# Modulation of the first mixer on TensorE strips, in a two-layer transformer trunk scheduled at build time

## The chip, the cores and the metric

The kernel runs on one core of a Trainium2 chip. Its time is device time in microseconds of one execution, as the median of the runs taken. The engines that matter are TensorE (PE in the profile, PEld its weight loads), VectorE (DVE), ScalarE (ACT) and GpSimd (POOL). SyncE (SP) issues the loads from DRAM.

## The reference

A trunk of two layers works on 512 tokens of 1024 features in float32. Each layer has a mixer and a gated feed-forward part, and each of these four sub-layers is modulated by a vector that depends only on the sequence:

```python
c_act = jax.nn.silu(c)
for l in range(DEPTH):
    mod = (c_act @ mod_w[l] + mod_b[l])[:, None, :]
    sh_m, sc_m, g_m, sh_f, sc_f, g_f = jnp.split(mod, 6, axis=-1)
    h = x * (1 + sc_m) + sh_m
    y = even_mixer(h, ...) if l % 2 == 0 else odd_mixer(h, ...)   # sparse and latent attention; stick-breaking attention
    x = layer_norm(DEEPNORM_ALPHA * x + (1 + g_m) * y, ln_mix_g[l], ln_mix_b[l])
    h = x * (1 + sc_f) + sh_f
    y = conv_ffn(h, ...)
    x = layer_norm(DEEPNORM_ALPHA * x + (1 + g_f) * y, ln_ffn_g[l], ln_ffn_b[l])
```

`mod` is the product of one row of 1024 numbers with a 1024 x 6144 matrix, so 6 parts of 1024 columns for each layer: shift, scale and gate of the mixer (parts 0, 1, 2) and of the feed-forward (3, 4, 5). The mixer of layer 0 cannot begin before parts 0 and 1 of layer 0 are there; part 2 is wanted at the end of its output projection, parts 3 and 4 at the start of the feed-forward.

## The kernel before

**How it is ordered.** The class `Plan` (L79 to L446) records every engine call in program order with its reads and writes. `schedule` then issues them as a list schedule: each engine takes the recorded operation with the lowest index plus `bias` among those that are ready by the plan's own prices (`price`, L200). Some calls are left open between engines: `nc.either` and `nc.lazy` record one operation for VectorE, GpSimd or ScalarE, and `worth` (L334) gives it to the engine that would finish first, after adding a `gain` in ns for GpSimd. `port` (L243) says which operations of VectorE and GpSimd hold the shared port and for which of them `worth` looks. In the trace every operation has the one line L446, in `emit`, so tiles are told by their names.

**Matmuls.** Most products are float32 split in two float32r parts, high and low, with three products (high-high, high-low, low-high). A weight tile `raw` is loaded, copied to its high part `whl` by ScalarE, and the low part is a subtraction on VectorE or GpSimd. `hl`, `h`, `qk`, `y`, `V` and `xres` are tiles of activations; `sc`, `tr`, `mm` and `md` are PSUM banks. A float32 product that is not split is carried out by TensorE as two instructions.

**The start** (L664 on) is a loop over the 8 blocks of 128 features. For block k two loads of 512 KB bring the columns of parts 0 and 1 (`y` from `in_m_dram`), another brings the transposed input, two more the weights of the first projection. The modulation is summed over 8 rows `r` of the loaded tile: ScalarE scales two (`y<-y,ca`, `ca` being silu(c)), GpSimd adds these (`xres<-y`), VectorE adds the other six, scaled, in one after another (`xres<-y,ca,xres`), and TensorE sums the 128 partitions in two products with a column of ones (`md<-ones,xres`). VectorE forms `A` and `B` from it, then `t = x A + B`; `h` is its high part (ScalarE) and low part (VectorE). 21 products of 128x512 into seven banks follow per block.

**Parts 2, 3 and 4 of layer 0** are computed by `mod_gate(0)` and `mod_cols(1)` while the rotary embeddings, index scores, top-k masks, latent projections and latent attention run. 48 loads of 256 KB (`mraw` from `in_mod_w_dram`, two buffers) are scaled and added to the tile `acc` by GpSimd (`mraw<-mraw,ca`, then `acc<-acc,mraw`), or in one instruction by VectorE; products with ones (`md<-ones,acc` for columns, `md<-acc,ones` for a gate that is wanted on all partitions) sum the partitions. Their bias is `MOD_BIAS` = 1560.

After them come the sparse attention, the first output product with its norm (`out_proj`), the feed-forward (`ffn_up` and the second output product), then layer 1 with the third and fourth output products. In an output product token tiles end one after another: gate, residual, norm, transposition by TensorE, `A` and `B`, the next `h`.

Of the kernel before, what the change touches and what calls it, by code (L numbers as in the profile page):

```python
# [20 lines left out]
P = 128  # L21
D = 1024
S = 512
# [31 lines left out]
# ns from the end of an instruction to the start of one that waits for it  # L55
# [14 lines left out]
# what each hold of the SBUF ports shared by VectorE and GpSimd waits for  # L70
# [8 lines left out]
class Plan:  # L79
    """Records engine calls in program order and issues them in the order of a list schedule.  # L80

    Dependences are those of the recorded order (by tile and region); a tag's tiles take
    their buffers in the recorded order, so the schedule cannot run out of buffers where
    the recorded order does not.
    """

    def __init__(self, nc):
# [11 lines left out]
        self.either = _Either(self, -200.0)  # L99
        self.lazy = _Either(self, -1020.0)  # L100
# [11 lines left out]
    # -- recording --  # L112
# [86 lines left out]
    # -- costs --  # L199
    def price(self, op):  # L200
# [42 lines left out]
    def port(self, op, e=None):  # L243
        """how an op holds the pair of SBUF ports that VectorE and GpSimd share"""
# [15 lines left out]
    # -- scheduling --  # L260
    def schedule(self):
# [21 lines left out]
        def offer(i):  # L283
            """op i has all its inputs; it can run once its new tiles have buffers"""
# [32 lines left out]
        def port_free(i, e):  # L317
            """when the pair of SBUF ports that VectorE and GpSimd share is free for op i"""
# [15 lines left out]
        def worth(i, e):  # L334
            """whether engine e would finish op i before any other that may run it"""
# [20 lines left out]
        def pe_time(op):  # L356
            """the time of a TensorE instruction at the clock that its activity allows"""
# [12 lines left out]
        while done < len(ops):  # L370
# [41 lines left out]
            op.start = clock[e]  # L412
            k = self.port(op)
# [35 lines left out]
class _Either:  # L449
    """Operations that several engines may run, whichever comes to it first."""  # L450
# [14 lines left out]
    def scale(self, out, src, by):  # L465
        """out = src * by, a column"""
# [3 lines left out]
    def norm(self, x, mean, scale, bias):  # L470
        """x = (x - mean) * scale in place; bias = -mean * scale"""
# [1162 lines left out]
```

## Time and profile before

| | us |
|---|---|
| median of 3 runs | 1408.58 (1407.68 to 1410.41) |
| profiled execution, span of its trace | 1414.6 |
| TensorE busy | 1337.3 (95%) |
| VectorE busy | 1102.1 (78%) |
| ScalarE busy | 727.8 (51%) |
| GpSimd busy | 333.9 (24%) |

The profiled execution has no time of its own beside its span; the span is 6.0 us above the median of the runs. Busy time sums the instructions of an engine, pipelined matmuls merged; shares are of the span. GpSimd's 333.9 us lie mostly in the first 385 us. The clock column of a stretch is the share of full speed that the throttle granted TensorE, 1.00 being 2.4 GHz and 0.50 being 1.2 GHz, as a mean over the stretch.

### The profile page before, as it was taken

How to read it: one execution, taken by the hardware profiler on the slowest of the kernel's cores; microseconds unless marked ns; L12 is line 12 of the kernel's file. 1: busy time of each engine (PE TensorE's matmuls, PEld its weight loads, DVE VectorE, ACT ScalarE, POOL GpSimd, SP SyncE). 2: the span in 40 equal slices, each digit the busy share in tenths (PEclk: the TensorE clock that was granted, in tenths of full speed). 3: DMA queues.
4: the chain of work that ended last, by engine and by line, in shares of the span. 5: the costliest groups of instructions: out<-in, count | busy, mean ns of one | idle time of the engine just before them, and what ended most of it. 6: DMA issues, size and time to landing. Idle time of an engine off the chain costs nothing.

```text
span 1414.6 us, 21212 instructions
## 1 busy us (share of the span) xinstructions
PE 1337.3 (95%) x7468; PEld 1131.9 (80%) x7468; DVE 1102.1 (78%) x2030; ACT 727.8 (51%) x1376; POOL 333.9 (24%) x311
## 2 busy tenths in 40 slices
PE   4888799999899999999999999999969999999997
PEld 3666577887788999888877888878858999998885
DVE  6997997789898888883485886777688889994347
ACT  4355566753544444443334886788344555564230
POOL 4575866623611111020040100100041000020000
PEclk9987888999999999999999999999989999999999
DMA  9422433254155444553412243321305323242331
GB/s 323 149 66 65 131 97 107 90 165 134 60 165 170 133 156 153 174 168 107 134 42 93 75 146 112 108 82 60 104 30 176 116 98 120 89 150 93 101 105 59
DMA packets 88458, 166.54 MB, mean 118 GB/s; under 512 B 11128, under 2 KB 13688, under 8 KB 88352
## 3 DMA queue, kind: packets, MB, share of 16 engines
q1 hardware_dynamic: 88064, 165.14, 37.2%
q8 instruction: 58, 0.95, 0.3%
q14 instruction: 48, 0.39, 0.1%
q10 hardware_dynamic: 288, 0.06, 0.0%
HBM read 158.80 MB, written 2.10 MB: 114 GB/s over the span
## 4 chain that ended last, share of the span: by engine, by line
PE 71%; DVE 14%; issue 4%; ACT 4%; DMA 4%; POOL 2%; SPq 0%; DVEq 0%; POOLq 0%; ACTq 0%
PE sc L446 38%; PE tr L446 16%; PE mm L446 13%; PE md L446 4%; DVE t L446 4%; DVE xres L446 2%; DVE row L446 2%; ACT t L446 2%; DMA raw<-in_wup_dram 1%; DVE h L446 1%; DVE acc L446 1%; ACT qk L446 1%; DMA mraw<-in_mod_w_dram 1%; DVE hl L446 1%; DVE st L446 1%
## 5 line engine op out<-in xcount | busy, mean ns | idle before, releaser
L446 PE MATMUL sc<-h,whl 128*128 128x512 f32 (+1 forms) x2076 | 422.8, 359 | 7.8 <-ACT h L446 4.7
L446 PEld LDWEIGHTS sc<-h,whl 128*128 128x128 f32 x2076 | 348.7, 194 | 63.5 <-ACT h L446 5.5
L446 ACT CAST whl<-raw 128x512 fp32r<-128x512 f32 (+1 forms) x352 | 213.4, 613 | 264.0 <-PE sc L446 154.6
L446 DVE TENSOR_TENSOR whl<-raw,whl 128x512 fp32r<-128x512 f32 x296 | 207.8, 709 | 109.4 <-ACT whl L446 107.9
L446 POOL TENSOR_TENSOR whl<-raw,whl 128x512 fp32r<-128x512 f32 (+1 forms) x77 | 105.5, 1379 | 476.3 <-ACT whl L446 325.9
L446 DVE SCALAR_TENSOR_TENSOR acc<-mraw,ca,acc 128x512 f32<-128x512 f32 x118 | 98.0, 831 | 14.0 <-DMA mraw<-in_mod_w_dram 13.1
L446 POOL TENSOR_TENSOR rs<-rs,nhalf 128x1 f32<-128x1 f32 (+1 forms) x19 | 14.3, 754 | 328.5 <-DVE rs L446 328.4
L446 PE MATMUL sc<-whl,t 128*128 128x512 f32 x252 | 67.4, 393 | 0.3 <-ACT t L446 0.3
L446 ACT ACTIVATE t<-t 128x512 f32<-128x512 f32 x84 | 52.7, 637 | 19.5 <-DVE t L446 19.1
L446 DVE TENSOR_TENSOR raw<-raw,raw 128x512 f32<-128x512 f32 x86 | 59.1, 688 | 4.3 <-DMA raw<-in_wup_dram 2.8
L446 PE MATMUL mm<-h,whl 128*128 128x512 f32 x204 | 60.2, 435 | 1.2 <-ACT y L446 1.2
L446 ACT ACTIVATE t<-t,rs 128x512 f32<-128x512 f32 x16 | 13.0, 815 | 90.9 <-DVE rs L446 90.8
L446 PEld LDWEIGHTS sc<-whl,t 128*128 128x128 f32 x252 | 47.1, 188 | 11.3 <-DVE t L446 0.7
L446 PEld LDWEIGHTS mm<-h,whl 128*128 128x128 f32 x204 | 42.1, 212 | 11.5 <-ACT y L446 1.7
L446 ACT CAST hl<-t 128x512 fp32r<-128x512 f32 (+1 forms) x74 | 44.7, 627 | 5.4 <-DVE t L446 4.9
L446 PE MATMUL mm<-hl,V 128*128 128x128 f32 (+5 forms) x342 | 45.7, 276 | 1.2 <-ACT hl L446 0.9
L446 PEld LDWEIGHTS mm<-hl,V 128*128 128x128 f32 (+1 forms) x342 | 39.0, 168 | 8.0 <-ACT hl L446 2.1
L446 PE MATMUL tr<-whl,t 128*128 128x512 f32 x168 | 43.2, 391 | 0.0
L446 PE MATMUL mm<-whl,t 128*128 128x512 f32 x168 | 43.0, 391 | 0.0
L446 DVE SCALAR_TENSOR_TENSOR xres<-y,ca,xres 128x256 f32<-128x256 f32 x48 | 36.6, 773 | 8.0 <-POOL xres L446 7.2
L446 PE MATMUL tr<-h,whl 128*128 128x256 f32 (+1 forms) x240 | 40.1, 315 | 2.5 <-POOL whl L446 1.6
L446 PE MATMUL sc<-y,h 96*128 96x128 f32 (+3 forms) x96 | 34.4, 470 | 7.6 <-ACT y L446 3.2
(388 smaller groups left out, 2976.6 us busy)
## 6 DMA issues: line engine op xcount, KB each, us to landing
raw<-in_wup_dram SPq DMA_DIRECT2D x176, 256.0 KB, 3.4
mraw<-in_mod_w_dram SPq DMA_DIRECT2D x160, 256.0 KB, 2.9
raw<-in_wdown_dram SPq DMA_DIRECT2D x88, 256.0 KB, 2.9
y<-in_m_dram SPq DMA_DIRECT2D x16, 512.0 KB, 7.2
raw<-in_w_out_dram SPq DMA_DIRECT2D x32, 256.0 KB, 2.6
raw<-in_wqk_dram SPq DMA_DIRECT2D x32, 256.0 KB, 3.0
row<-in_ln_dram SPq DMA_DIRECT2D x8, 512.0 KB, 4.0
raw<-in_wqkv_dram SPq DMA_DIRECT2D x16, 256.0 KB, 3.0
```

Of the source, the lines that this page charges most:

```text
L446: getattr(getattr(self.nc, op.eng), op.fn)(*op.args, **op.kw)
```

## The change

**Start.** `ca` becomes column 0 of `cab`, a tile of 32 columns of which 31 are zero. For each block, 8 float32 matmuls take `cab[:, r, :]` (32 columns) as stationary operand and 256 modulation columns as moving one. Row r goes to partitions 32 (r mod 4) on, so four lie in one group of column positions each. ScalarE copies the 128x256 result, and the same two products with ones sum the partitions. VectorE's six additions, ScalarE's two scalings and GpSimd's addition go.

**Parts 2, 3, 4 of layer 0.** `first_gate` and `first_cols` replace `mod_gate(0)` and `mod_cols(1)`. Each of the 48 loads feeds two strips (`md<-mraw,cab`), which add up in PSUM. The gate's four row pieces get the bias, which four small loads bring, and are spread over all partitions by four products; the columns are obtained by four transposes. `MOD_BIAS` is 200.

**Engines and order.** GpSimd's `gain` goes from -200 and -1020 to 9000 ns up to the first output product, from 390 to 2000 until layer 1's attention, where it stays 500, and from 840 to 9000 for `either` after it. The price of a float32r product becomes the longer of its streaming plus 13 ns (7 up to 64 columns) and 0.859 ns a stationary column; a strip is priced at a quarter of its streaming; the start of a VectorE or GpSimd operation waits in the plan for `port_free`. The bias of `token_sums` falls from 670 to 100. `ones` shrinks to one column that is broadcast, `negs` from 15 to 12 columns. Docstrings and comments go too.

```diff
-        self.either = _Either(self, -200.0)
-        self.lazy = _Either(self, -1020.0)
+        self.either = _Either(self, 9000.0)
+        self.lazy = _Either(self, 9000.0)
...
+            if size(lhs) == COLS:
+                op.work /= P // COLS
+                return op.work + 2.5
...
-            return max(op.work + 2.5, size(lhs) * (1.6667 if lhs.dtype == F32 else 0.835))
+            return max(op.work + (13.0 if size(lhs) > 64 else 7.0), size(lhs) * 0.859)
...
+            if e in ("vector", "gpsimd"):
+                op.start = clock[e] = max(clock[e], port_free(i, e))
...
-        for r in range(MV_SPLIT, 8):
-            nc.scalar.mul(row(r), row(r), ca[:, r:r + 1])
-            if r > MV_SPLIT:
-                nc.gpsimd.tensor_tensor(acc[:, 1, :], row(r), acc[:, 1, :] if r > MV_SPLIT + 1 else row(MV_SPLIT), ALU.add)
-        nc.vector.scalar_tensor_tensor(acc[:, 0, :], row(0), ca[:, 0:1], acc[:, 1, :], ALU.mult, ALU.add)
-        for r in range(1, MV_SPLIT):
-            nc.vector.scalar_tensor_tensor(acc[:, 0, :], row(r), ca[:, r:r + 1], acc[:, 0, :], ALU.mult, ALU.add)
+        for r in range(KD):
+            g = r % 4
+            nc.tensor.matmul(cs[COLS * g:COLS * g + COLS, 0:256], lhsT=cab[:, r, :], rhs=m0[r // 4][:, g, :], start=r < 4, stop=r >= 4, skip_group_check=True)
+        rk = xa[:, 1, 0:256]
+        nc.scalar.copy(rk, cs[:, 0:256])
...
-    TOPK_BIAS, MOD_BIAS = 1500.0, 1560.0
+    TOPK_BIAS, MOD_BIAS = 1500.0, 200.0
...
+    def strips(o, l, part, at):
+        for r in range(KD):
+            for half in range(2):
+                m = tl("mraw", [P, S])
+                nc.sync.dma_start(m[:], t["mod_w"][l, r * P:(r + 1) * P, part * D + half * S:part * D + (half + 1) * S])
+                for i in range(2):
+                    g = 2 * half + i
+                    nc.tensor.matmul(o[COLS * g:COLS * g + COLS, at:at + 256], lhsT=cab[:, r, :], rhs=m[:, 256 * i:256 * i + 256], start=r == 0, stop=r == KD - 1, skip_group_check=True)
...
-    drain([mod_gate(0), mod_cols(1)])
+    first_gate()
+    first_cols()
...
-            nc.bias = 670.0
+            nc.bias = 100.0
...
-    nc.either.gain, nc.lazy.gain = (390.0, -180.0)
+    nc.either.gain, nc.lazy.gain = (2000.0, -180.0)
...
-    nc.either.gain, nc.lazy.gain = (840.0, 410.0)
+    nc.either.gain, nc.lazy.gain = (9000.0, 410.0)
```

In the issue order of TensorE, one step of the start reads as follows before: `md<-ones,xres` are the two sums over partitions for the next block, all others products of the current one.

```order
L446 MATMUL md_99<-ones,xres_118 128x1 x2
L446 MATMUL tr_94<-h_91,whl_111 128x512
L446 MATMUL tr_95<-h_91,whl_111 128x512 x3
L446 MATMUL mm_96<-h_91,whl_112 128x512 x3
L446 MATMUL sc_97<-h_91,whl_112 128x512 x3
L446 MATMUL mm_98<-h_91,whl_112 128x512 x3
```

The same place after, where `md_100<-y_125,cab` are four strips of a later block.

```order
L454 MATMUL sc_93<-h_92,whl_112 128x512
L454 MATMUL md_100<-y_125,cab 32x256 x4
L454 MATMUL sc_93<-h_92,whl_112 128x512 x2
L454 MATMUL sc_94<-h_92,whl_112 128x512 x3
L454 MATMUL md_100<-y_126,cab 32x256 x4
L454 MATMUL tr_95<-h_92,whl_112 128x512 x3
L454 MATMUL tr_96<-h_92,whl_112 128x512
L454 MATMUL md_100<-ones,xres_127 128x1 x2
L454 MATMUL tr_96<-h_92,whl_112 128x512 x2
L454 MATMUL mm_97<-h_92,whl_113 128x512 x3
L454 MATMUL sc_98<-h_92,whl_113 128x512 x2
L454 MATMUL md_100<-y_133,cab 32x256 x4
```

Each block's two groups of four strips now stand singly between products, two to three blocks ahead of the products that need them.

On VectorE, one step of the start before: the additions of the modulation lie around `A`, `B`, `t` and `h`.

```order
L446 SCALAR_TENSOR_TENSOR A_77<-md_99,mbT 128x1
L446 TENSOR_TENSOR B_81<-md_99,mbT 128x1
L446 TENSOR_SCALAR t_48_131<-xres_126,A_77,B_81 128x512
L446 SCALAR_TENSOR_TENSOR xres_134<-y_132,ca,xres_134 128x256 x2
L446 TENSOR_TENSOR h_91<-t_48_131,h_91 128x512
L446 SCALAR_TENSOR_TENSOR xres_134<-y_132,ca,xres_134 128x256
L446 SCALAR_TENSOR_TENSOR xres_134<-y_133,ca,xres_134 128x256 x2
```

And after, where two subtractions of the weights `whl`, GpSimd's before, stand with `A`, `B`, `t` and `h`.

```order
L454 TENSOR_TENSOR whl_128<-raw_130,whl_128 128x512
L454 SCALAR_TENSOR_TENSOR A_78<-md_100,mbT 128x1
L454 TENSOR_TENSOR B_82<-md_100,mbT 128x1
L454 TENSOR_TENSOR whl_129<-raw_131,whl_129 128x384
L454 TENSOR_SCALAR t_48_132<-xres_127,A_78,B_82 128x512
L454 TENSOR_TENSOR h_92<-t_48_132,h_92 128x512
```

No addition of the modulation is left there, and the step has six instructions.

On TensorE at the first latent score (`sc<-y,h`), before: projections, then scores, with no modulation between them.

```order
L446 MATMUL sc_435<-h_333,whl_433 128x512 x9
L446 MATMUL sc_438<-h_333,whl_436 128x512 x6
L446 MATMUL sc_435<-h_333,negs 128x512 x2
L446 MATMUL sc_442<-y_439,h_333 128x128
L446 MATMUL sc_438<-y_439,negs 128x512
L446 MATMUL sc_438<-y_440,negs 128x512
L446 MATMUL sc_443<-y_440,h_333 128x128
L446 MATMUL sc_442<-y_439,h_333 128x128 x2
```

And after, where `md_341<-mraw_351,cab` is the pair of strips of one load.

```order
L454 MATMUL sc_431<-h_334,whl_429 128x512 x6
L454 MATMUL md_341<-mraw_351,cab 32x256 x2
L454 MATMUL sc_431<-h_334,whl_429 128x512 x2
L454 MATMUL sc_434<-h_334,whl_432 128x512 x6
L454 MATMUL md_341<-mraw_352,cab 32x256 x2
L454 MATMUL sc_431<-h_334,negs 128x512 x2
L454 MATMUL sc_438<-y_435,h_334 128x128
L454 MATMUL sc_434<-y_435,negs 128x512
L454 MATMUL sc_434<-y_436,negs 128x512
L454 MATMUL md_341<-mraw_353,cab 32x256 x2
L454 MATMUL sc_439<-y_436,h_334 128x128
L454 MATMUL sc_438<-y_435,h_334 128x128 x2
```

All 48 pairs stand ahead of the first sparse score, 11 of them ahead of the first latent score, 37 between the two; the sums of the partial sums are gone from there.

## Rows read from the trace of the kernel before

**Rows 1.** Busy time by stretches: us, PE, PEld, DVE, ACT, POOL (x instructions), clock

```profile
17.50:72.60 55.10, 50.11 (x203) 38.57 (x204) 50.62 (x87) 19.83 (x39) 28.18 (x23) 1.00 0.61 205
72.60:168.00 95.40, 81.04 (x311) 59.43 (x309) 83.11 (x154) 51.33 (x97) 71.28 (x57) 0.82 0.29 81
168.00:251.40 83.40, 75.61 (x445) 59.92 (x446) 71.00 (x194) 55.13 (x136) 53.10 (x64) 0.84 0.38 105
251.40:359.20 107.80, 106.11 (x700) 86.17 (x700) 91.07 (x244) 59.80 (x153) 45.47 (x53) 1.00 0.41 130
...
385.00:1010.00 625.00, 619.02 (x3393) 526.85 (x3392) 470.08 (x773) 349.06 (x617) 72.42 (x57) 0.99 0.40 125
```

**Rows 2.** Timeline of TensorE, first sums and product: start us, us, what [idle before]

```profile
14.40 1.01 PE L446 MATMUL md<-ones,xres 128*128 128x1 f32 x4 [14.40 <-DVE xres L446]
17.52 2.09 PE L446 MATMUL sc<-h,whl 128*128 128x512 f32 x4 [2.11 <-ACT h L446]
```

**Rows 3.** Timeline of ScalarE, first modulation rows

```profile
7.67 0.91 ACT L446 ACTIVATE y<-y,ca 128x256 f32<-128x256 f32 x2 [2.47 <-DMA y<-in_m_dram]
```

**Rows 4.** Timeline of TensorE, one k-step of the start

```profile
36.58 0.61 PE L446 MATMUL md<-ones,xres 128*128 128x1 f32 x4 [0.19 <-DVE xres L446]
37.05 1.19 PE L446 MATMUL tr<-h,whl 128*128 128x512 f32 x4
...
40.14 1.52 PE L446 MATMUL sc<-h,whl 128*128 128x512 f32 x6
...
42.65 0.49 PE L446 MATMUL md<-ones,xres 128*128 128x1 f32 x3 [0.54 <-DVE xres L446]
```

**Rows 5.** Timeline of VectorE, same step

```profile
38.29 1.00 DVE L446 SCALAR_TENSOR_TENSOR xres<-y,ca,xres 128x256 f32<-128x256 f32 x2
...
39.81 3.92 DVE L446 SCALAR_TENSOR_TENSOR xres<-y,ca,xres 128x256 f32<-128x256 f32 x4
```

**Rows 6.** Timeline of GpSimd, same step

```profile
40.85 2.61 POOL L446 TENSOR_TENSOR whl<-raw,whl 128x512 fp32r<-128x512 f32 x2
```

**Rows 7.** Groups by shape, GpSimd, 72 to 252 us: busy us, mean ns | idle before

```profile
L446 POOL TENSOR_TENSOR acc<-acc,mraw 128x512 f32<-128x512 f32 x23 | 29.4, 1278 | 3.0 <-DMA acc<-in_mod_b_dram 1.8
...
L446 POOL TENSOR_TENSOR whl<-raw,whl 128x512 fp32r<-128x512 f32 x9 | 13.3, 1479 | 8.5 <-DVE whl L446 4.9 <-ACT whl L446 2.1 <-DVE iwt L446 1.6
```

**Rows 8.** Groups by shape, VectorE, 72 to 252 us

```profile
L446 DVE TENSOR_TENSOR hl<-t,hl 64x512 fp32r<-64x512 f32 x4 | 6.3, 1579 | 0.1
...
L446 DVE TENSOR_TENSOR hl<-tr,hl 128x512 fp32r<-128x512 f32 x6 | 3.9, 681 | 0.5 <-ACT hl L446 0.5
```

**Rows 9.** Timeline of TensorE, float32 products of 512 columns

```profile
445.41 0.84 PE L446 MATMUL sc<-h,whl 128*128 128x512 f32 x3
446.09 1.02 PE L446 MATMUL md<-acc,ones 128*128 128x512 f32 x2
446.54 2.18 PE L446 MATMUL sc<-h,whl 128*128 128x512 f32 x7
```

**Rows 10.** Timeline of TensorE, products in two halves of the rows

```profile
853.94 0.49 PE L446 MATMUL mm<-row,qk 64*128 64x512 f32 x1
853.95 0.49 PE L446 MATMUL sc<-row,qk 64*128 64x512 f32 x1
854.37 1.20 PE L446 MATMUL sc<-whl,h 128*128 128x512 f32 x4
```

**Rows 11.** The tile of modulation weights, 140 to 340 us: who waited, us, times

```profile
  DMA mraw<-in_mod_w_dram: 13.8, 13
```

**Rows 12.** Groups by shape, TensorE, 251.4 to 359.2 us

```profile
L446 PE MATMUL md<-ones,acc 128*128 128x1 f32 x30 | 4.4, 249 | 0.4 <-DVE acc L446 0.4
```

**Rows 13.** Timeline of TensorE, first and third output product

```profile
362.64 0.62 PE L446 MATMUL tr<-h,whl 128*128 128x256 f32 x3 [1.57 <-POOL whl L446]
...
1051.90 0.90 PE L446 MATMUL sc<-ident,t 128*128 128x128 f32 x3 [7.16 <-DVE t L446]
```

**Rows 14.** Timeline of VectorE, third output product

```profile
1042.23 3.09 DVE L446 TENSOR_TENSOR h<-t,h 128x512 fp32r<-128x512 f32 x2
```

More of the change, by code (lines that the diff above doesn't have):

```diff
@@ L21 @@
 P = 128
+COLS = 32
 D = 1024
@@ L628, in tile_trunk @@
     nc.sync.dma_start(cT[:], t["cT"])
-    ca = const("ca", [P, KD])
-    nc.scalar.activation(ca[:], cT[:], AF.Silu)
+    cab = const("cab", [P, KD, COLS])
+    nc.vector.memset(cab[:], 0.0)
+    nc.scalar.activation(cab[:, :, 0], cT[:], AF.Silu)
+    ca = cab[:, :, 0]
+    heads = const("heads", [P, 4])
+    nc.vector.memset(heads[:], 0.0)
+    for g in range(4):
+        nc.vector.memset(heads[COLS * g:COLS * g + 1, g:g + 1], 1.0)
     mbT = const("mbT", [P, 12, KD])
@@ new lines, in first_cols @@
+    def first_cols():
+        lng, lnb = lnT[:, 0, :], lnT[:, 1, :]
+        o = bank("md")
+        for what in range(2):
+            strips(o, 0, 3 + what, 256 * what)
+        x = tl("acc", [P, S])
+        nc.scalar.copy(x[:], o[:])
+        o = bank("md")
+        for j in range(4):
+            nc.tensor.transpose(o[:, j * P:(j + 1) * P], x[:, j * P:(j + 1) * P], ident[:])
+        cols = o[:].rearrange("p (w a g r) -> p w g a r", w=2, a=2, r=COLS)[:, :, :, :, 0]
+        got = []
+        for what in range(2):
+            c = small([P, KD], tag="mc", bufs=4)
+            nc.vector.tensor_tensor(c[:].rearrange("p (g a) -> p g a", a=2), cols[:, what], mbT[:, 3 + what, :].rearrange("p (g a) -> p g a", a=2), ALU.add)
+            got.append(c)
+        sh, sc = got
+        nc.vector.tensor_scalar(sc[:], sc[:], 1.0, None, ALU.add)
+        nc.vector.tensor_tensor(A_col[1][:], sc[:], lng, ALU.mult)
+        nc.vector.tensor_tensor(sc[:], sc[:], lnb, ALU.mult)
+        nc.vector.tensor_tensor(B_col[1][:], sc[:], sh[:], ALU.add)
@@ new lines, in first_gate @@
+    def first_gate():
+        o = bank("md")
+        strips(o, 0, 2, 0)
+        x = tl("acc", [P, S])
+        nc.gpsimd.memset(x[:, 0:256], 0.0)
+        for g in range(4):
+            nc.sync.dma_start(x[COLS * g:COLS * g + 1, 0:256], t["mod_b"][0:1, 2 * D + g * 256:2 * D + (g + 1) * 256])
+        nc.vector.tensor_tensor(x[:, 0:256], o[:, 0:256], x[:, 0:256], ALU.add)
+        gate = tl("gate", [P, D])
+        gates[0] = gate
+        for half in range(2):
+            o = bank("md")
+            for i in range(2):
+                g = 2 * half + i
+                nc.tensor.matmul(o[:, 256 * i:256 * i + 256], lhsT=heads[:, g:g + 1].broadcast_to((P, P)), rhs=x[:, 0:256], start=i == 0, stop=i == 1, skip_group_check=True)
+            nc.scalar.activation(gate[:, half * S:(half + 1) * S], o[:], AF.Identity, bias=ones[:, 0:1])
@@ L1112, in tile_trunk @@
         0: [tuple(va[:, i, j, :] for i in range(2)) for j in range(NT)],
-        1: [tuple(negs[:, 3 + 4 * i + j:5 + 4 * i + j, :].rearrange("p a b -> p (a b)") for i in range(2)) for j in range(NT)],
+        1: [tuple(negs[:, 4 * i + j:2 + 4 * i + j, :].rearrange("p a b -> p (a b)") for i in range(2)) for j in range(NT)],
     }
```

42 lines of the change are left out of this document (21 added, 21 removed).

## The prediction, made before the changed kernel was run

> **What bounds the kernel now.** I read the busy time by stretches first [rows 1]. From 385 to 1010 us TensorE is busy 619.02 of 625.00 us, so nothing that GpSimd or VectorE does there can matter until it makes TensorE wait. The change has to act before 385 us and in the two tails of the output products. The reader should see three different stretches ahead of that. From 17.5 to 72.6 us, the start, VectorE (50.62) and TensorE (50.11) are equally busy. From 72.6 to 168 us VectorE is at 83.11 of 95.40 and GpSimd at 71.28, while TensorE, busy 81.04, is granted a clock of 0.82. From 168 to 251.4 us nobody is full: TensorE 75.61 of 83.40 at 0.84, VectorE 71.00, GpSimd 53.10. From 251.4 to 359.2 us TensorE is busy 106.11 of 107.80: there it is the bound.
>
> Next I read one k-step of the start on TensorE [rows 4]: the sums of the modulation start at 36.58 and again at 42.65, 6.07 us apart, and the second start waited 0.54 us for VectorE. Then the reason on VectorE and GpSimd [rows 5, 6]: two scaled additions 128x256 end after 1.00 us, but four of them take 3.92 us while GpSimd's subtractions run beside them, about 0.98 each instead of 0.50. The same stretching is in the groups of 72 to 252 us [rows 8]: a 64x512 subtraction takes 1579 ns where a 128x512 one, whose input lies on PSUM, takes 681.
>
> **The sum.** It is made against the profiled execution, whose span is 1414.6 us. The median of the timed runs, 1408.6, lies 6.0 below it, and I take 6.0 off at the end. A change under 0.2% (2.8 us) is what a measurement here cannot tell from none. Two unknowns decide: q, what a group of four strips costs TensorE in the start, and p, what a pair costs it later.
>
> *Price of a strip.* No row of before shows a matmul with 32 stationary columns. A float32 128x512 product is two TensorE instructions; between 445.41 and the end at 448.72 two of them stand among ten products [rows 9]. Ten products at 0.227 from start to start (six from 40.14 to 41.50 [rows 4]), the last one with its full 0.39, leave about 0.87, so 0.43 each. A strip moves half the columns in two such instructions: 0.43 alone. Four one behind another are 1.71, two are 0.85. If strips in different column groups run side by side, a group or a pair takes 0.43 (a pair then fills half the array, a group all of it). The nearest rows to such sharing are two 64-row products in different halves of the array [rows 10]: they start at 853.94 and 853.95 and last 0.49 each, so they run together, and the next full product starts 0.42 later where streaming alone wants 0.227. Sharing exists, and about 0.2 goes on the change to and fro. I take q = p = 0.63, by that row, and keep 0.43 and the serial 1.71 and 0.85 as ends.
>
> The Trainium skill, TensorEngine Tiling (Array Packing), Key Properties, says that changing the tiling mode (not just the tile) drains TensorE; it speaks against putting 64 groups and pairs singly between full products, and the 0.42 for 0.227 in [rows 10] agrees in direction. The skill's TensorE: Matmul & The Clock Gate, Measured speedup vs the span model, has four row tiles at 3.07 times one after another and column tiles nearly alike; by it a group would be an estimated 0.56, which would make the sum about 3.5 us lower.
>
> *Start.* Removed per k: six VectorE additions, two ScalarE scalings, one GpSimd addition. Added: eight strips and one ScalarE copy of 128x256; VectorE takes GpSimd's two weight subtractions (about 0.6 and 0.5 at plain speed), far less than the 4.9 that go, so its cover is large and I cost it at nothing. The first product started at 17.52, behind a sum that waited until 14.40 for VectorE [rows 2], though the first modulation rows had landed at 7.67 [rows 3]: VectorE's six additions lay between. Two groups of strips and a copy take about 3 us there, so the first product starts some 3.8 us earlier. Against that, six groups come while products still run at half clock, each 0.43 dearer: 2.6. Net -1.2. For the seven later steps the 0.54 wait goes and two groups come: 7 x (2q - 0.54). Together T1 = 14q - 5.0; with 0.63 that is +3.8, with 0.43 +1.0. That the strips are in time rests on loads: a k's strips stand two to three steps ahead of its products.
>
> *72.6 to 251.4 us.* GpSimd is busy 124.4 there, of which modulation is 45 (its largest group 29.4 [rows 7]); 80 us of subtractions, rotations and scalings move to VectorE, where the same forms take half (681 against 1479 [rows 7, 8]). That is about 22 us more for VectorE before 168 and 15 after. What it gains is the stretching: its groups at their plain durations would be about 20 and 11 us shorter (four 64x512 subtractions alone give 3.6). So it goes from 83 to 86, and from 71 to 75. Before 168 it had 12.3 us of idle, mostly behind TensorE and ScalarE; I let 6 stay: 91.4 for 95.4, -4, between +3 (all idle stays) and -9 (none). The 11 pairs that stand before the first latent score lie under VectorE's work and cost nothing. After 168, TensorE's 445 instructions at their warm spacings are 58 us (75.61 at clock 0.84 gives 63.5 as the other end); 37 pairs come between the first latent score and the first sparse one, and 6 of the 7.8 idle stay: 58 + 6 + 37p against 83.4, so -19.4 + 37p, but not under -3.4, where VectorE's 75 and its 5 of idle bind. With 0.63, +3.9. T2 = -0.1. This counts on the full clock: the wait for GpSimd's products goes, TensorE is busier, and 83.4 at 0.84 becomes a stretch at 1.00 like the one behind it [rows 1]. If it stays at 0.84, up to 6 us are lost.
>
> *251.4 to 359.2 us.* The 30 small products of the partial sums [rows 12] go, at a spacing of 0.47 / 4 [rows 4] 3.5 us, with a wait of 0.4: T3 = -4, between 0 and -6.
>
> *Tails.* In the first output product TensorE waits 1.57 for a GpSimd subtraction [rows 13], and the gate is ready long before: -3 with two smaller waits. In the third it waits 7.16 at 1051.90 for VectorE [rows 13], at the end of a chain in which two subtractions took 3.09 us together beside GpSimd [rows 14]; plain they take half: -2. T4 = -5, between 0 and -8.
>
> Elsewhere the subtractions that leave GpSimd add about 35 us (half of GpSimd's 72.42) to VectorE's 470.08 of 625 [rows 1]: hidden by TensorE, and priceless until VectorE is late for a weight. The shorter constants and the other biases I cost at nothing under the same cover; with it gone they are a few tenths.
>
> Forecast: 3.8 - 0.1 - 4 - 5 = -5.3; 1414.6 - 5.3 - 6.0 = **1403 us**.
>
> **Rivals.** *Full sharing (q = p = 0.43).* The change of groups costs nothing: the rows show its price only for groups of rows, none for groups of columns. T1 = +1.0, T2 = -4 - 3.4, then -9: -15.4, 1393 us. Against it: 0.42 for 0.227 in [rows 10].
>
> *No sharing (q = 1.71, p = 0.85): slower.* One mechanism: a strip is two instructions that add into the same columns, and if TensorE starts each only when the one before has streamed its 256 columns, a group costs four strips. Place: the start, where TensorE has no idle to hide them, 7 steps of 2 groups, and the stretch after 168 us. T1 = 18.9, T2 = -4 + 12.1, -9: +18, 1427 us. It decides once q and p pass about 0.73 together (14q - 5 - 23.4 + 37p = 9). The rows show sharing only of single-pass products in halves of rows, not of float32 in columns, so it keeps a fair chance.
>
> *Half sharing (q = 1.27, p = 0.84).* A strip's second instruction waits for its first, but overlaps the next strip's first, with the 0.2 on top: T1 = 12.8, T2 = -4 + 11.7, -9: +11.5, 1420 us.
>
> *The queue.* Strips stand in TensorE's order and wait there for their load. In before, 13 waits for modulation weights cost GpSimd, ScalarE and VectorE 13.8 us together [rows 11] and TensorE next to nothing; the tile still has two buffers. If all of it moves to TensorE with the forecast's prices: -5.3 + 13.8, 1417; by half, 1410, no change. Against: the loads are issued as early as buffers come free, and strips free them within 1 us where GpSimd held one for 2 (1.278 for its addition alone [rows 7], after a scaling).
>
> **Chances.** Forecast 0.37, full sharing 0.25, none 0.15, half 0.13, the queue 0.10. The forecast's own range is 1397 to 1409 (the ends of T2 and T4), so a tenth of the whole from it is within 0.2% and nearly none slower; half of the queue's is. Faster 0.57, same 0.13, slower 0.30. The range of 8 in 10, from full sharing with somewhat more gained in the tails to no sharing without the upper tail: 1387 to 1425.
>
> **What would show it.** In the profile after, strips of a group starting within a few ns and the next product 0.6 after the group's first: q right; 0.43: full sharing; starts 0.2 apart through the group: none. First product near 13.7. Steps of the start 6.8 apart. TensorE's clock 1.00 from 168 us on, with VectorE busy near 75 there and its 64x512 subtractions near 680 ns: T2 right; 1579 still: the stretching has another cause than GpSimd. TensorE idle behind a modulation load of over 5 us in all: the queue. Idle at the third output product still over 6: T4 wrong. Times above 1411 would mean that strips cost more than the waits they replace.

## The result and the profile after

The changed kernel takes 1421.7 us (1412.1 to 1427.9, nine runs) where the kernel before took 1408.6 (1407.4 to 1410.6): a ratio of 1.0091, 95% interval 1.0070 to 1.0113. It is slower by 13 us; forecast were 1403 us and a gain. The profiled execution spans 1422.8 us and took 1424.6 as timed, 1.8 more than its span.

Stretches by work are compared below, cut at the same instructions in both kernels: the first product, the last product of the start, the first and the last latent score, the first product of the first feed-forward, the first of layer 1's projections, its attention, the third output product, its last transposed product, and the first product of the last output product. The view is busy time by stretches, with columns as in [rows 1]. After:

```profile
11.90:73.20 61.30, 61.30 (x331) 42.73 (x332) 36.95 (x80) 25.37 (x51) 0.00 (x0) 1.00 0.66 227
73.20:148.50 75.30, 69.88 (x332) 47.85 (x330) 66.57 (x158) 40.81 (x79) 3.73 (x3) 1.00 0.47 130
148.50:255.20 106.70, 100.97 (x599) 66.79 (x599) 83.11 (x239) 59.81 (x146) 0.00 (x0) 0.84 0.40 113
255.20:402.70 147.50, 141.68 (x943) 120.41 (x942) 124.38 (x304) 85.50 (x197) 31.67 (x29) 0.99 0.27 83
402.70:610.60 207.90, 203.27 (x1287) 183.73 (x1285) 175.70 (x310) 96.04 (x167) 5.96 (x5) 1.00 0.52 159
610.60:742.60 132.00, 130.23 (x579) 106.33 (x580) 79.66 (x136) 45.48 (x80) 16.99 (x14) 1.00 0.34 107
742.60:1045.10 302.50, 292.62 (x1538) 240.48 (x1537) 219.93 (x373) 206.19 (x371) 23.96 (x24) 0.99 0.31 94
1045.10:1076.40 31.30, 24.07 (x178) 23.18 (x178) 28.06 (x46) 16.53 (x31) 9.48 (x8) 0.84 0.19 58
1076.40:1292.30 215.90, 211.64 (x1435) 195.82 (x1434) 190.60 (x339) 113.59 (x200) 2.60 (x3) 0.99 0.39 122
```

And before, cut at the same work:

```profile
17.50:76.20 58.70, 53.71 (x219) 41.57 (x220) 54.22 (x89) 21.04 (x41) 31.70 (x25) 1.00 0.59 197
76.20:168.00 91.80, 77.44 (x295) 56.43 (x294) 79.51 (x152) 50.12 (x95) 67.76 (x55) 0.81 0.29 81
168.00:251.10 83.10, 75.31 (x443) 59.89 (x444) 71.00 (x194) 54.84 (x134) 52.87 (x63) 0.84 0.38 105
251.10:405.70 154.60, 147.71 (x974) 124.61 (x973) 133.39 (x303) 84.26 (x194) 70.13 (x70) 0.98 0.38 120
405.70:609.30 203.60, 201.84 (x1286) 183.34 (x1284) 174.62 (x293) 96.45 (x167) 23.53 (x19) 1.00 0.51 161
609.30:741.40 132.10, 131.69 (x581) 106.69 (x582) 81.20 (x131) 46.12 (x81) 24.78 (x18) 1.00 0.34 106
741.40:1038.80 297.40, 291.96 (x1537) 240.28 (x1535) 219.15 (x372) 204.21 (x368) 25.91 (x24) 0.99 0.31 96
1038.80:1074.10 35.30, 25.87 (x177) 24.28 (x176) 31.79 (x51) 19.08 (x33) 14.16 (x11) 0.81 0.23 71
1074.10:1284.10 210.00, 209.66 (x1435) 194.94 (x1434) 187.02 (x325) 111.49 (x198) 12.59 (x9) 1.00 0.37 122
```

The reader should see two halves. Up to the first feed-forward the changed kernel is ahead by 3 us (402.7 against 405.7), though GpSimd does next to nothing: the start ends 3 us earlier, the stretch up to the first latent score is 16.5 shorter, the latent stretch 23.6 longer, the rest 7.1 shorter. Two executions cannot carry these sizes alone. In the runs e4 and e14 below all engines keep the order of before up to some 327 us, and the start ends at 74.7 us in both (76.2 above) and the latent stretch at 245.4 and 247.8 (251.1 above). In e15 and e1 TensorE keeps the order of the changed kernel beyond 300 us, and the latent stretch ends at 248.9 and 248.2 (255.2 above). One order thus varies by 6 us there; the mean lead of three executions each at the first feed-forward is still 2.8 us (399.2 against 402.0), though their plans part after 306 us. From 402.7 on it loses 4.3 in the feed-forward, 5.1 in layer 1's attention, 5.9 in the second feed-forward, and wins 4.0 in the tail of the third output product. TensorE has idle there that it had not before: 207.90 less 203.27 is 4.6 where before it was 1.8, and 302.50 less 292.62 is 9.9 where it was 5.4.

*The strips.* The timeline of TensorE after, in the start and in the latent stretch:

```profile
35.10 0.64 PE L454 MATMUL md<-y,cab 128*32 128x256 f32 x8
35.67 0.96 PE L454 MATMUL mm<-h,whl 128*128 128x512 f32 x3
36.47 0.63 PE L454 MATMUL sc<-h,whl 128*128 128x512 f32 x2
...
40.48 0.40 PE L454 MATMUL tr<-h,whl 128*128 128x512 f32 x1
40.81 0.64 PE L454 MATMUL md<-y,cab 128*32 128x256 f32 x8
...
198.11 0.63 PE L454 MATMUL md<-mraw,cab 128*32 128x256 f32 x4
198.67 0.96 PE L454 MATMUL sc<-h,whl 128*128 128x512 f32 x3
...
218.45 1.07 PE L454 MATMUL md<-mraw,cab 128*32 128x256 f32 x4
219.45 1.01 PE L454 MATMUL sc<-y,h 96*128 96x384 f32 x2
```

Eight instructions are four strips. Their first instructions start within 20 ns, the second ones 0.24 us later, and the next full product 0.57 after the first (35.10 to 35.67): the four run side by side. The last product ahead of a group takes 0.33 to it (40.48 to 40.81) instead of 0.227. The first product behind a group is late too: three products take 0.80 (35.67 to 36.47), not 0.68. A group of four therefore costs 0.57 + 0.10 + 0.11 = 0.78 us among full products at the upper clock, and a pair 0.77 (0.56 from 198.11 to 198.67, with the same 0.10 and 0.11 where products of 128x512 stand on both sides). The Trainium skill, TensorE: Matmul & The Clock Gate, The mechanism, has row tiles starting some 4 ns apart; these column tiles start 6 to 7 ns apart in the trace. At half clock the pair takes 1.00 (218.45 to 219.45).

*The start.* The first product stood at 17.52 [rows 2]; now, from the timeline of TensorE:

```profile
11.88 0.79 PE L454 MATMUL sc<-h,whl 128*128 128x512 f32 x1
12.60 1.08 PE L454 MATMUL md<-y,cab 128*32 128x256 f32 x8
...
19.91 0.64 PE L454 MATMUL md<-y,cab 128*32 128x256 f32 x8
20.48 0.50 PE L454 MATMUL tr<-h,whl 128*128 128x512 f32 x1
```

It starts at 11.88. The group at 12.60 still takes 1.0 to the next product; from the one at 19.91 on it is 0.57. In before TensorE idled until 14.40, and its products still start 0.40 apart from 27.91 to 29.11, so the faster spacing comes some 9 us earlier now. The clock column reads 1.00 for the start in both kernels; the two speeds are read from the spacings.

*VectorE.* The group of VectorE from 73 to 255 us that stood at 1579 ns in [rows 8]:

```profile
L454 DVE TENSOR_TENSOR hl<-t,hl 64x512 fp32r<-64x512 f32 x4 | 2.7, 686 | 0.6 <-ACT hl L454 0.6
```

With GpSimd busy 3.73 us between 73.2 and 255.2, it takes what the 128x512 subtraction of [rows 8] takes, 681. The prediction named this as the sign that GpSimd caused the stretching.

*The clock.* Busy time at the second pair of heads, cut every 5 us:

```profile
170.00:175.00 5.00, 5.00 (x35) 3.19 (x32) 4.52 (x13) 2.27 (x4) 0.00 (x0) 1.00 0.39 108
175.00:180.00 5.00, 3.81 (x28) 1.97 (x26) 3.85 (x10) 3.25 (x6) 0.00 (x0) 1.00 0.70 206
180.00:185.00 5.00, 4.00 (x23) 2.12 (x21) 3.89 (x12) 2.56 (x8) 0.00 (x0) 0.82 0.57 161
185.00:190.00 5.00, 5.00 (x22) 3.38 (x22) 3.27 (x12) 2.65 (x9) 0.00 (x0) 0.50 0.36 105
```

TensorE is idle for 1.2 and 1.0 us in the second and third row, and in the fourth it is at 1.2 GHz (0.50). The whole latent stretch stands at 0.84, just as before.

*Tail of the third output product.* In [rows 13] TensorE waited 7.16 us; now 5.17:

```profile
1056.23 1.12 PE L454 MATMUL sc<-ident,t 128*128 128x128 f32 x4 [5.17 <-DVE t L454]
```

### The profile page after: what moved, and what is told of

It reads as the page before. It is cut to its first block, busy times and chain, and to the rows that moved or that the text cites. A ratio compares the mean times of both kernels' runs of the same rounds, so it can differ in the third digit from the quotient of the medians.

```text
span 1422.8 us, 21450 instructions
## 1 busy us (share of the span) xinstructions
PE 1361.0 (96%) x7764; PEld 1127.9 (79%) x7764; DVE 1070.7 (75%) x2105; ACT 726.7 (51%) x1380; POOL 97.8 (7%) x95
## 4 chain that ended last, share of the span: by engine, by line
PE 46%; DVE 13%; DMA 6%; ACT 4%; issue 4%; POOL 0%; DVEq 0%; POOLq 0%; ACTq 0%
PE sc L454 23%; PE tr L454 11%; PE mm L454 9%; DVE t L454 4%; DMA mraw<-in_mod_w_dram 3%; PE md L454 3%; DMA raw<-in_wup_dram 3%; DVE acc L454 2%; DVE whl L454 2%; ACT t L454 1%; DVE raw L454 1%; DVE row L454 1%; ACT qk L454 1%; DVE h L454 0%; ACT whl L454 0%
## 5 line engine op out<-in xcount | busy, mean ns | idle before, releaser
L454 ACT CAST whl<-raw 128x512 fp32r<-128x512 f32 (+2 forms) x351 | 212.3, 614 | 256.3 <-PE sc L454 147.7
L454 DVE TENSOR_TENSOR whl<-raw,whl 128x512 fp32r<-128x512 f32 (+1 forms) x344 | 231.7, 682 | 130.6 <-ACT whl L454 125.9
L454 DVE SCALAR_TENSOR_TENSOR acc<-mraw,cab,acc 128x512 f32<-128x512 f32 x104 | 79.6, 765 | 18.9 <-DMA mraw<-in_mod_w_dram 18.0
L454 POOL TENSOR_TENSOR whl<-raw,whl 128x512 fp32r<-128x512 f32 x29 | 42.7, 1479 | 371.0 <-DVE B L454 167.6
L454 DVE TENSOR_TENSOR raw<-raw,raw 128x512 f32<-128x512 f32 x92 | 63.5, 690 | 6.2 <-DMA raw<-in_wup_dram 4.5
L454 PE MATMUL mm<-h,whl 128*128 128x512 f32 x204 | 55.8, 404 | 0.7 <-ACT y L454 0.7
L454 PEld LDWEIGHTS sc<-whl,t 128*128 128x128 f32 x252 | 47.3, 188 | 10.7 <-ACT t L454 0.4
L454 ACT CAST hl<-t 128x512 fp32r<-128x512 f32 (+1 forms) x77 | 46.7, 625 | 10.6 <-DVE t L454 9.0
L454 PEld LDWEIGHTS mm<-h,whl 128*128 128x128 f32 x204 | 37.1, 188 | 12.4 <-issue 4.6
L454 ACT CAST hl<-tr 128x128 fp32r<-128x128 f32 (+3 forms) x64 | 26.1, 425 | 36.7 <-PE tr L454 36.2
L454 DVE TENSOR_TENSOR hl<-tr,hl 128x128 fp32r<-128x128 f32 (+3 forms) x64 | 30.1, 486 | 15.2 <-ACT hl L454 15.0
L454 DVE TENSOR_TENSOR hl<-t,hl 128x512 fp32r<-128x512 f32 (+1 forms) x44 | 29.4, 689 | 15.6 <-ACT hl L454 11.1
```

Of the source, the lines that this page charges most:

```text
L454: getattr(getattr(self.nc, op.eng), op.fn)(*op.args, **op.kw)
```

## The experiments

Theory L, formed on the profile: the loss is in the later stages because GpSimd was shut out of them and VectorE is late. Rival S: the strips and the half clock they meet make the loss. Rival P: it is the plan's new prices. All ratios are to the kernel before, measured beside.

| run | what it is | us | ratio (95%) |
|---|---|---|---|
| e1 | after, late gains and token bias of before | 1426.9 | 1.0147 (1.0115 to 1.0178) |
| e4 | before, late gains and token bias of after | 1407.1 | 0.9994 (0.9978 to 1.0010) |
| e2 | after, old prices, no port wait | 1408.9 | 1.0019 (0.9991 to 1.0048) |
| e6 | before, strips in the start, new prices | 1429.8 | 1.0159 (1.0131 to 1.0188) |
| e7 | before, strips in the start, old prices | 1409.7 | 1.0028 (1.0014 to 1.0042) |
| e8b | before, new product price | 1429.0 | 1.0162 (1.0144 to 1.0179) |
| e8c | before, port wait in the plan | 1427.0 | 1.0150 (1.0130 to 1.0170) |
| e9 | after, no port wait | 1432.0 | 1.0179 (1.0158 to 1.0200) |
| e10 | after, old product price | 1418.5 | 1.0071 (1.0041 to 1.0101) |
| e15 | after, old product price from the first output product on | 1407.9 | 1.0016 (0.9998 to 1.0034) |
| e16 | after, old product price up to there | 1419.7 | 1.0113 (1.0076 to 1.0150) |
| e11 | before, product 0.5 ns dearer | 1421.3 | 1.0093 (1.0067 to 1.0118) |
| e12 | after, other engines' prices 5% up | 1416.8 | 1.0061 (1.0040 to 1.0082) |
| e13 | e2, gain 840 after the third output product | 1409.6 | 1.0015 (0.9987 to 1.0043) |
| e14 | e4, gain 840 there | 1407.1 | 0.9992 (0.9979 to 1.0005) |
| e17 | e13, strips of parts 2 to 4 in fours | 1397.1 | 0.9933 (0.9917 to 0.9949) |
| e18 | after, strips in fours | 1408.7 | 1.0015 (0.9995 to 1.0034) |
| e19 | e15, strips in fours, gain 840 | 1402.2 | 0.9961 (0.9939 to 0.9982) |

**Gains and biases or prices.** The edits of e1 and e4 (reversed):

```diff
-    nc.either.gain, nc.lazy.gain = (2000.0, -180.0)
+    nc.either.gain, nc.lazy.gain = (390.0, -180.0)
...
-            nc.bias = 100.0
+            nc.bias = 670.0
...
-    nc.either.gain, nc.lazy.gain = (9000.0, 410.0)
+    nc.either.gain, nc.lazy.gain = (840.0, 410.0)
```

> Changed kernel with the settings of before from the first output product on (gains 390 and 840, token_sums bias 670). Theory L (the loss is VectorE being late there, once GpSimd is left out): the three stretches 403-610, 760-1045 and 1077-1292 us give back most of their 15 us, so 1407 to 1412 us. Rival S (strips at half clock and their waits make the whole loss, the late part is chance): 1418 to 1425, within 0.3% of the changed kernel.

> Kernel before with only the late settings of the changed one (2000 and 9000 ns, token_sums bias 100). Theory L: 8 to 15 us slower than before, 1417 to 1424. Rival S: within 0.3% of before, 1405 to 1413.

Theory L fell as the account of the whole loss, on both sides: giving the old settings back made it no faster (1426.9), and the new ones on the kernel before cost nothing (1407.1). The stretches say more than the sum. In e4's trace the second feed-forward takes 216.5 us instead of 210.0; in the changed kernel it takes 215.9, and in e1, with the old gains, 212.8. TensorE waits there for VectorE's `acc`, 3.5 us in e4 and 3.4 in the changed kernel, against 0.3 before. So this one loss goes with the late gain, as theory L has it. In e4 the attention of 294.2 us (297.4 before) and the tail of 31.5 (35.3) make up for it, and the attention by chance: in e14 TensorE keeps e4's order up to 1098 us and takes 297.4 for it, with 6.8 us at half clock that e4 does not have. The wait in the changed kernel (us in all, times, longest), then by stretches the attention of e4 and of e14 and the second feed-forward of e4:

```profile
PE md L454 <- DVE acc L454: 3.4, 2, 3.0
```

```profile
733.40:1027.60 294.20, 288.85 (x1537) 238.33 (x1535) 218.71 (x372) 204.10 (x368) 25.82 (x24) 1.00 0.30 96
735.27:1032.62 297.35, 291.98 (x1536) 240.21 (x1535) 218.87 (x372) 204.23 (x368) 25.84 (x24) 0.99 0.32 96
1059.10:1275.60 216.50, 211.95 (x1436) 195.89 (x1435) 190.15 (x337) 112.05 (x201) 6.16 (x5) 0.99 0.37 123
```

The edit of e2:

```diff
-            if lhs.dtype == F32:
-                return max(op.work + 2.5, size(lhs) * 1.6667)
-            return max(op.work + (13.0 if size(lhs) > 64 else 7.0), size(lhs) * 0.859)
+            return max(op.work + 2.5, size(lhs) * (1.6667 if lhs.dtype == F32 else 0.835))
...
-            if e in ("vector", "gpsimd"):
-                op.start = clock[e] = max(clock[e], port_free(i, e))
```

> Changed kernel with the prices of before (float32r product 2.5 ns over its streaming, no wait for the port when an operation starts in the plan). Theory L holds the gains to blame, so this stays within 0.4% of the changed kernel, 1416 to 1427. Rival P (the new prices make the plan believe that weights are ready when they aren't): 1408 to 1413.

Rival P held: 1408.9, with all strips and gains in place. Rival S falls with it as the whole cause; that the strips have a cost of their own is shown at the end. e6 and e7 are the kernel before with the start of the changed one, by the new and the old prices; seen from the changed kernel, beside the edits of e1 (and, in e7, e2):

```diff
-        self.either = _Either(self, 9000.0)
-        self.lazy = _Either(self, 9000.0)
+        self.either = _Either(self, -200.0)
+        self.lazy = _Either(self, -1020.0)
...
-    TOPK_BIAS, MOD_BIAS = 1500.0, 200.0
+    TOPK_BIAS, MOD_BIAS = 1500.0, 1560.0
...
-    first_gate()
-    first_cols()
+    drain([mod_gate(0), mod_cols(1)])
```

> Strips in the start alone: parts 2, 3 and 4 by vector sums, gains and biases as before, the new prices kept. If the start gains by itself what its traces show (-3 us at the end of the start) and the prices do nothing: 1403 to 1407. If strips cost more than they free there: 1409 or more.

> Kernel before with strips in the start alone and the old prices. The same with the new prices took 1429.8. If the prices are the whole of that loss: 1402 to 1408, the start's own 3 us gained. If the strips in the start have a part in it: above 1412.

1429.8 against 1409.7: 20 us from the prices. The second lies between its two answers: by the old prices the strips in the start gain nothing. The start ends at 75.7 us in e7 and at 72.6 in e6; against 76.2 both look like gains, against the 74.7 of e4 and e14, in before's order, e7's is none.

**Which price.** e8b and e8c put one each into the kernel before; e9 and e10 take one each out of the changed one (the first and the second hunk of e2's edit).

> Kernel before with only the new price of a float32r product (streaming plus 13 or 7 ns, 0.859 a column). Theory PP (the new product price alone makes the later stages slower, whatever the modulation): 1416 to 1424. Rival PW (it is the wait for the port in the plan): 1404 to 1410, no change. Rival X (the price hurts only together with strips): no change here and in the next.

> Kernel before with only the wait for the port when a VectorE or GpSimd operation starts in the plan. Theory PP: 1404 to 1410, no change. Rival PW: 1414 to 1422.

> Changed kernel without the wait for the port in the plan, the new product price kept. Theory PP: stays at 1417 to 1425. Rival PW: 1405 to 1412.

> Changed kernel with the old price of a product throughout and the port wait kept. Theory M: 1407 to 1413, like the one without the port wait (1408.9). Rival O: 1416 or more.

Either alone costs the kernel before 21 to 23 us, and the changed one keeps some 10 us or more over e2 while one of them is left, so neither theory was right alone. In layer 1's attention it is the product price: 300.6 (e8b) and 300.7 us (e9), against 294.0 in e8c and e10, all four without a stretch at half clock there. The same holds in the first feed-forward, 207.4 and 208.4 us against 203.0 and 203.6: in all twenty traces it takes 205.8 us or more where the new price holds there, and 204.8 or less where it does not. The port wait shows in the stretch that is 609 to 741 us in before: 138.1 us in e8c, 132.6 in e8b; but the changed kernel, which has it too, takes 132.0 there.

**Where the price acts.** In e15 and e16 a flag picks the old price for the operations recorded after, or before, the line that sets the gains for the first output product.

```diff
+            if getattr(self, "slim", False):
+                return max(op.work + 2.5, size(lhs) * 0.835)
             return max(op.work + (13.0 if size(lhs) > 64 else 7.0), size(lhs) * 0.859)
...
     nc.either.gain, nc.lazy.gain = (2000.0, -180.0)
+    nc.slim = True
```

> Changed kernel with the old price of a product from the first output product on only. Theory M (exact prices take the lead that operands had over TensorE; seen as idle of TensorE in the first feed-forward, 4.6 us for 0.3 to 1.8, and in layer 1's attention, 9.9 for 5.4): these two stretches give back 7 to 9 us, 1411 to 1416. Rival O (any plan but the one the settings were fitted to is late somewhere): 1418 or more.

> Changed kernel with the old price of a product up to the first output product only. Theory M: the late stretches stay as in the changed kernel (feed-forward 207.8, layer 1's attention 302.5), 1416 to 1424. If the early stages hold the harm: 1407 to 1413.

This is the clearest of the runs. Up to 306 us TensorE's instructions stand in the same order in both kernels, so only the later plan differs, and 1421.7 becomes 1407.9 (13.8 us between the medians, 10.6 by the two ratios to before). At one mean clock, 0.985, the changed kernel took 1419.5 us and e15 1406.9 and 1404.0, so the lower clock of some runs does not make the difference. Its stretches, first feed-forward to second, as above:

```profile
396.70:599.40 202.70, 202.10 (x1286) 183.27 (x1284) 176.23 (x305) 96.29 (x167) 15.22 (x12) 1.00 0.51 165
599.40:731.70 132.30, 131.29 (x584) 107.58 (x585) 78.97 (x136) 46.17 (x81) 14.41 (x13) 1.00 0.33 106
731.70:1028.80 297.10, 291.55 (x1534) 239.74 (x1532) 220.27 (x373) 205.31 (x371) 22.72 (x23) 0.99 0.31 95
1028.80:1060.60 31.80, 24.11 (x178) 23.21 (x177) 28.86 (x49) 18.70 (x33) 11.03 (x9) 0.84 0.17 53
1060.60:1274.30 213.70, 212.39 (x1436) 195.40 (x1435) 186.18 (x331) 112.45 (x198) 8.93 (x7) 1.00 0.38 124
```

207.9 has become 202.7, 302.5 is 297.1, 215.9 is 213.7; together 12.8 us. The two profiled spans differ by 18.0; the 6.0 us ahead of the first feed-forward fall almost whole where the order is the same, and are no effect of the edit. What TensorE waits for in layer 1's attention (us in all, times, longest), before, after and in e15:

```profile
PE mm L446 <- ACT hl L446: 1.3, 5, 0.4
```

```profile
PE mm L454 <- ACT hl L454: 3.3, 4, 1.2
PE mm L454 <- issue: 1.5, 1, 1.5
```

```profile
PE mm L456 <- issue: 1.5, 1, 1.5
PE mm L456 <- ACT hl L456: 1.1, 4, 0.4
```

With the new price 3.3 us are waited for ScalarE's copy `hl`, with the old one 1.3 and 1.1. That is 2 of the 5 us; the rest is spread over small waits. e16, with the new price late, stays slow. So does e10, which has e15's price late but another plan early; its runs go from 1409.6 us at a mean clock of 0.985 to 1426.4 at 0.970. The terms do not simply add up.

**How big the price must be.** Theory M: the old price, 215.9 ns for a product that starts every 0.227 us in the trace, kept the plan's TensorE some 5% faster than the real one, so operands were ready early; the new one, 213.4 of streaming and 13, so 226.4, is nearly exact and takes this lead. Rival O: the settings fit one order of instructions, and any other costs some 20 us.

```diff
-            return max(op.work + 2.5, size(lhs) * (1.6667 if lhs.dtype == F32 else 0.835))
+            return max(op.work + (2.5 if lhs.dtype == F32 else 3.0), size(lhs) * (1.6667 if lhs.dtype == F32 else 0.835))
```

> Kernel before with a product priced 0.5 ns dearer (0.2%). Theory M (the size of the price matters: 2.5 ns over streaming keeps the plan's TensorE faster than the real one, and so operands early): no change, 1403 to 1410. Rival O (the other settings of the kernel fit one order of instructions only, and any other order costs some 20 us): 1415 or more, or at least 1% off.

The edit of e12, in the changed kernel:

```diff
     def price(self, op):
+        c = self.price1(op)
+        return c * 1.05 if op.eng in ("vector", "scalar", "gpsimd") else c
+
+    def price1(self, op):
```

> Changed kernel with every price of VectorE, ScalarE and GpSimd raised by 5%, about what the new product price took from their lead over TensorE. Theory M: the later stages get back their 9 us, 1405 to 1414. Rival O: 1418 or more.

Both theories fell as stated: e11 lies where O had it, e12 between the two. Half a nanosecond costs 13.6 us, far too much for M; and seven kernels with quite other orders (e2, e4, e7, e13, e14, e15, e18) stand within 0.3% of before, so O is false too. e12 got back layer 1's attention (294.1) and the second feed-forward (211.2), as M has it, but its first feed-forward took 212.9. M may describe layer 1's attention; why e11 loses what it loses stays open: its profile has 4.8 us after the first feed-forward begins, the rest is not visible in one execution.

**The gain after the third output product**, in e2 (e13) and in e4 (e14):

```diff
     h, xres = out_proj(2, t["w_out1"], yT, xres, rows)
+    nc.either.gain = 840.0
```

> Changed kernel with the old prices and no port wait, and the gain of either back at 840 after the third output product. The second feed-forward was 5 to 6 us longer in every kernel with 9000 there. Additive: 1401 to 1405. If plans do not add up: 1409 or more.

> Kernel before with the late settings of the changed one (2000, 9000 in the third output product, token_sums bias 100) but 840 after that product. In the traces the settings took 3 us off layer 1's attention and 3.8 off the tail and added 6 in the feed-forward; additive: 1398 to 1402. If plans do not add up: 1405 or more.

Plans did not add up: the 4 us that the second feed-forward gives back (216.5 to 212.5 in e14) were not seen in the median. The 3 us that e14's expectation counts for layer 1's attention were e4's luck with the clock, shown above.

**Strips in fours.** A pair costs as much as four. e17 and e18 record both loads of a row first and make each strip wait in the plan for the second:

```diff
+            ms = [tl("mraw", [P, S]) for _ in range(2)]
             for half in range(2):
-                m = tl("mraw", [P, S])
-                nc.sync.dma_start(m[:], t["mod_w"][l, r * P:(r + 1) * P, part * D + half * S:part * D + (half + 1) * S])
-                for i in range(2):
-                    g = 2 * half + i
-                    nc.tensor.matmul(o[COLS * g:COLS * g + COLS, at:at + 256], lhsT=cab[:, r, :], rhs=m[:, 256 * i:256 * i + 256], start=r == 0, stop=r == KD - 1, skip_group_check=True)
+                load = nc.sync.dma_start(ms[half][:], t["mod_w"][l, r * P:(r + 1) * P, part * D + half * S:part * D + (half + 1) * S])
+            for g in range(4):
+                op = nc.tensor.matmul(o[COLS * g:COLS * g + COLS, at:at + 256], lhsT=cab[:, r, :], rhs=ms[g // 2][:, 256 * (g % 2):256 * (g % 2) + 256], start=r == 0, stop=r == KD - 1, skip_group_check=True)
+                op.deps.add(load.idx)
```

> Old prices, no port wait, 840 after the third output product (1409.6 with pairs), and the strips of parts 2 to 4 in groups of four: both halves of a row of weights are awaited, then four strips go together. A pair and a group of four each cost TensorE 0.66 us in the trace, so 48 pairs become 24 groups, 16 us of TensorE less between 73 and 255 us. If that work is what eats the gain: 1395 to 1403. If VectorE or the loads bind there: 1405 to 1412.

> Changed kernel with strips of parts 2 to 4 in fours and nothing else. If grouping and prices add up (grouping took 12.5 us off the kernel with old prices): 1407 to 1412, and runs within 6 us of one another instead of 16. If the prices decide alone: 1418 or more.

> Changed kernel with strips in fours, the old price of a product from the first output product on, and 840 after the third. Additive: 1407.9 less 12, 1394 to 1399, as the one with old prices throughout (1397.1) or somewhat below. If plans do not add up: 1402 or more.

Fours take 13.0 us off the changed kernel (e18) and 12.5 off e13 (e17), or 10.7 and 11.5 by the ratios. e17 beats both kernels: 1397.1 us, 0.9933 of before. e18's runs still spread over 14 us (1404.0 to 1418.2), so the hoped-for narrowing is e17's alone (1395.2 to 1399.5). e19 fell short of adding up. The groups of TensorE from 73 to 255 us, after and in e17, and e17's timeline at one group:

```profile
L454 PE MATMUL md<-mraw,cab 128*32 128x256 f32 x192 | 32.8, 430 | 5.2 <-DMA mraw<-in_mod_w_dram 5.2
```

```profile
L450 PE MATMUL md<-mraw,cab 128*32 128x256 f32 x192 | 21.9, 426 | 6.3 <-DMA mraw<-in_mod_w_dram 6.3
```

```profile
163.65 0.64 PE L450 MATMUL md<-mraw,cab 128*32 128x256 f32 x8
164.22 0.91 PE L450 MATMUL mm<-hl,V 128*128 128x128 f32 x9
```

The busy time of the strips falls from 32.8 to 21.9 us. Eight instructions take 0.57 (163.65 to 164.22), as four did.

## Why the prediction was wrong

**The mechanism of a strip was right, its size too small.** q and p were taken as 0.63 by [rows 10]; they measure 0.78 and 0.77. The sum counted 0.2 for the change to and fro; it is 0.35: 0.10 on the product ahead, 0.14 between the group's 0.43 and the next product, 0.11 on the product behind. By the prediction's own formula this is past its mark of 0.73: q = p = 0.78 gives T1 = +5.9, T2 = +5.5 and a sum of +2.4, so 1411 us and no gain. None and half sharing are out, since the starts lie within 20 ns; full sharing is out, since a group costs 0.78 and not 0.43.

**T1 (start, +3.8 forecast) came out at -3.0**, or -1.5 against the starts of e4 and e14. A step is 6.8 us as forecast: 5.71 from 35.10 to 40.81 with 16 products, and 5 more at 0.227. That is luck: two groups cost 0.3 more than forecast, and the sums over partitions with their wait cost as much less than [rows 4] had them. Two smaller terms were wrong: the first product came 5.6 us earlier, not 3.8, and two groups ran at half clock after it, not six.

**T2 (73 to 255 us, -0.1 forecast) came out at +7.1**, 174.9 to 182.0 us. By the other executions in the two orders (170.7 and 173.1 in e4 and e14, 175.1 and 175.0 in e15 and e1) it is some 4.5 on the mean of three. VectorE is busy 149.7 us there, less than the forecast 161, and 37 pairs at 0.77 are 28.5 us, where the sum had 23. The sentence that failed besides is "This counts on the full clock": the latent stretch stands at 0.84 still, and in e15, in the same order, at 0.90, where it takes 6.5 us less. How much of T2 is the pairs and how much the clock these runs do not part. Some of the queue rival is true: TensorE waited 5.2 us for modulation loads (the row of the changed kernel under strips in fours), just over the 5 that the prediction named as its sign, where [rows 11] had 13.8 for others.

**T3 and T4 (-4 and -5 forecast)** came out at -7.1 together up to the first feed-forward, and -4.0 in the third output product: as forecast or better.

So up to here the account is 3.0 + 7.1 + 4.0 - 7.1 = 7.0 us gained, where 5.3 was forecast. That the sum comes near is luck in part, as T1 and T2 missed in opposite directions.

**The failed step is "Elsewhere ... hidden by TensorE" and, in the same paragraph, "the other biases I cost at nothing".** The three later stretches lost 4.3 + 5.1 + 5.9 = 15.3 us. The first two, 9.4 us, come from an edit for which the sum had no term: the price of a product in the plan. In e8b, which puts it alone into the kernel before, they take 207.4 and 300.6 us (203.6 and 297.4 before); e15, which takes it back in the later stages alone, has 202.7 and 297.1 and is 13.8 us faster than the changed kernel. The price reorders every engine in stretches where TensorE is busy 97 to 99%, and there TensorE now idles 4.6 and 9.9 us, where it idled 1.8 and 5.4. The third stretch, 5.9 us, is what that paragraph weighed and put at nothing, GpSimd left out and VectorE late: it goes with the gain of 9000 and not with the price (216.5 in e4 with the old price, 210.8 in e8b with the new price and the old gain), and TensorE waits 3.4 us for VectorE there. Other things move it too: nine traces with 9000 there have 211.2 to 218.3 us, eleven with 840 have 209.3 to 215.4.

**The offset was wrong too.** The 6.0 us between span and median were no constant: timed executions take 1.7 to 2.1 us more than their span, so the profiled execution of before, by estimate 1414.6 + 1.8 = 1416.4, was a slow one, 7.8 over its median, and the sum against it was flattered. By the last latent score it was already 5.7 and 3.3 us behind e4 and e14, in the same order. Of the error of 18.4 us (1421.7 less 1403.3), the later stretches are 15.2 (15.3 less 0.1 in layer 1's projections), the offset 4.9 (6.0 less the 1.1 between span and median after), and -1.7 the better rest.

"Slower" had 0.30 in all, and its rivals named other mechanisms (strips one behind another or half so, and the queue). That a plan's prices are an edit like any other was in none of the cases. Against e17 the changed kernel carries two costs, each shown alone: the pairs (13.0 us, e18) and the prices (13.8 in the later stages, e15). The two do not add up: with both taken away e19 is at 1402.2, 6.5 us below e18. Why the plans of e8c and e11 lose as much as they do is not shown, and `MOD_BIAS` and the gains ahead of the first output product were not tested alone.

## What to carry to other kernels

Where a planner orders the work, a change of its prices is a change of every queue, and even a truer price can cost more than the operations that it comes with: give it a term of its own, with both signs, and measure it alone. Price a small matmul with its entry and exit (here 0.35 us beyond the streaming, 0.43), counted to the second product behind it, and fill each group before paying: four strips cost what two do. Take the offset between span and timed run from the profiled execution itself, not from the median, and read a stretch from several executions of one order before a difference of a few us is believed.

## What had not been expected of the hardware

With TensorE's instructions in the same order up to 306 us, the changed kernel and e15 came to the last latent score at 255.1 and 248.9 us. The latent stretch stands at 0.84 in the one (shown above) and at 0.90 in the other:

```profile
148.75:248.87 100.12, 95.86 (x598) 62.03 (x598) 81.62 (x237) 59.07 (x145) 0.00 (x0) 0.90 0.42 121
```

The nine runs of the changed kernel go by and large with their mean clock, from 1412.1 us at 0.988 to 1427.9 at 0.974, and those of e13 from 1401.6 at 0.983 to 1422.3 at 0.968. The granted clock of one stretch is thus no property of the order alone.
